# Wider projection streams, split low-rank stores and block-diagonal state products in a two-layer hybrid trunk

## The chip, the cores and the metric

The kernel runs on one core of a Trainium2 chip. The metric is the device time of one execution in microseconds (us). Three executions of the kernel before took 4823.67, 4823.92 and 4831.27 us, median 4823.92. All numbers below that are not one of these come from one further execution, taken with the hardware profiler; it took 4847.04 us, of which 4845.3 us lie between its first and last instruction (the span).

## The reference

Two layers follow each other. Each computes, for 256 context tokens and 2048 latent tokens of width 1024:

```
h  = rms_norm(x, norm_w) * (1 + scale) + shift          # scale, shift, gate from SiLU(c) @ mod_w
pa, pb, pt = split(h @ w_in)                            # 4096 columns: three head groups
ya = rwkv7(pa)      # 6 heads of 64, two directions: per token
                    #   sa = state @ -kk;  state = state * w + sa (x) b + v (x) k;  y = state @ r
                    #   decay and learning rate come through two low-rank maps of width 64
yb = hgrn2(pb)      # 4 heads of 64, two directions, gated linear recurrence
yt = windowed_attention(pt)                             # 6 query heads, 2 key heads, sinks, rotary
x  = x + gate * (concat(ya, yb, yt) @ w_out)
```

In layer 1 the RWKV value is also mixed with that of layer 0. A last RMSNorm ends the trunk. Everything is float32.

## The kernel before

Tokens are numbered 0 to 2303; the first 256 are context. Each layer has two phases.

**Phase 1, the input projection** (`inproj_phase`). `norm_block` normalises 256 tokens, transposes them on TensorE (PE) and writes them as a tile `h` of two parts, a rounded high part and the rest (`hi`, `lo`, type fp32r), with 1024 features along partitions. The weight is taken in tiles of 128 columns (32 in layer 0, 33 in layer 1), in an order `order`, and split the same way on GpSimd (`whi`, `wlo`). A product is 24 matmuls: whi and wlo against the high part and whi against the low part, for 8 slices of 128 features (L347, L348). The tokens go in two sweeps, `SWEEP`: blocks of 512, 256 (context) and 512 tokens, then two of 512. A block of 512 is two runs of 24 matmuls, one for each 256 tokens, into two halves of one PSUM tile `ps` (L344 to L349). ScalarE (ACT) copies `ps` out, VectorE (DVE) applies the centred shift into a tile `s` (two buffers), and `post` does what the column tile needs. Two kinds of column tile matter here:

- j = 9 and j = 10 are the low-rank columns of decay and learning rate, both directions in one tile: partitions 0 to 63 are the forward direction, 64 to 127 the backward one. `parts` (L517 to L529) rounds them into buffers `t` and stores these and the rest to a DRAM scratch `wa`, by DMAs from SyncE's queue (SP).
- j = 3, 4, 5 are RWKV's keys. `post` squares them on ACT into a buffer `t`, sums over heads with a matmul against `bones` into `pa` (L435), and scales with Ln and Exp through two more buffers `t`.

The buffers `t` are four (`CFG["tm"]`). The order of columns begins 9, 3, 10, 4, 0, 5. A preparation of RWKV's chunks (`RwkvPrep`, in windows of 256 tokens) is mixed into phase 1 from the eighth column on.

**Phase 2** (`phase2`) mixes RWKV's 36 chunk steps with HGRN windows, attention blocks and, near its end, the output projection (`Readout`, whose matmuls `opo` stream 512 columns of fp32r). A chunk has 64 tokens; z is the direction, p a pair of heads, hp the head in it. `RwkvSeq.step` is the recurrence: R = KZ against the state S0, `rs` = R + lk on DVE, U = XT against rs, four ACT copies of U into UV, Sn = bkt against UV, the new state on DVE, and the output Y. Before, each of R and U is 12 matmuls, one for each z, p and hp: `t.mm(R[r, z, p], KZ[:, z, 3 + p, hp], S0[:, z, p])`, `t.mm(U[r, z, p], XT[r, z, p], rs[r, z, p])`, where `r` is the head's half of the partitions. `XT` are the inverses of the chunk from the scratch `XD`; `load` fetches them two steps ahead into one of two buffers (L827).

The order on each engine is not the order of the code. A list scheduler with a timeline of its own places each instruction; the emission order, `high_priority` in `step` and the share of each stream in `phase2` steer it. Each engine then works through its list in order, SP's DMA issues too.

Of the kernel before, what the change touches and what calls it, by code (L numbers as in the profile page):

```python
# [46 lines left out]
class Trunk:  # L47
# [185 lines left out]
    def norm_block(self, l, src, tiles, t0, n):  # L233

        nc = self.nc
        h = self.hp.tile([128, 2, KD, BLK + 2], F32R, name="h", tag="h")
        hi, lo = h[:, 0, :, 0:n], h[:, 1, :, 0:n]
        mc = self.modc[l]
        which = 1 if t0 == 0 else 0
        for k in range(0, KD, 2):  # L240
            ps = self.pax.tile([128, 2, n], F32, name="pa", tag="pa")
            hf = self.np.tile([128, 2, n], F32, name="hf", tag="hf", bufs=CFG["hf"])
            for e in range(2):
                for i, x in enumerate(tiles):
                    self.tr(ps[:, e, i * 128:(i + 1) * 128], x[:, (k + e) * 128:(k + e + 1) * 128])
                s, bsh = mc[:, k + e, which, 0:1], mc[:, k + e, which, 1:2]
                self.ts(hf[:, e], ps[:, e], s, ALU.mult, bsh, ALU.add)
            self.act(hi[:, k:k + 2], hf, AF.Identity)
            self.tt(lo[:, k:k + 2], hf, hi[:, k:k + 2].bitcast(F32), ALU.subtract, nc.gpsimd if k >= CFG["nl"] else None)
        if t0 == 0:  # L250

            x, = self.normed(l, src, SWEEP[1][0][0], 2)
            ps = self.pax.tile([128, KD, 2], F32, name="pa", tag="pa")
            for k in range(KD):
                self.tr(ps[:, k], x[:, 128 * k:128 * k + 128])
            hf = self.np.tile([128, KD, 2], F32, name="hf", tag="hf", bufs=CFG["hf"])
            self.tt(hf, ps, mc[:, :, 0, 0:1].to_broadcast([128, KD, 2]), ALU.mult)
            self.tt(hf, hf, mc[:, :, 0, 1:2].to_broadcast([128, KD, 2]), ALU.add)
            hi, lo = h[:, 0], h[:, 1]
            self.act(hi[:, :, n:n + 2], hf, AF.Identity)  # L260
            self.tt(lo[:, :, n:n + 2], hf, hi[:, :, n:n + 2].bitcast(F32), ALU.subtract)
        return hi, lo


    def inproj_phase(self, l, src, prep, start):
# [7 lines left out]
        with ExitStack() as ph:  # L273
            pool = lambda name, bufs, **kw: self.pool(ph, f"{name}{l}", bufs, **kw)
            self.np, self.tmp = pool("np", 1), pool("tm", CFG["tm"])
            wrp, wsp = pool("wr", 1), pool("ws", 2)
            self.hp = pool("hp", 5)
            self.pbp, sbp, kp = pool("pb", 1), pool("sb", 2), pool("keep", 1)
            self.pax = pool("pa", 2, psum=True)
            self.pin = pool("pi", 3, psum=True)  # L280
# [36 lines left out]
            for sw in range(2):  # L317
# [4 lines left out]
                for pos, j in enumerate(order):  # L322
# [16 lines left out]
                    for t0, bn in SWEEP[sw]:  # L339
                        c0, c1 = BLK if skip and t0 == 0 else 0, BLK + 2 if shifted and t0 == 0 else BLK  # L340
                        if c0 >= c1:
                            continue
                        ps = self.pin.tile([128, 512], F32, name="ps", tag="ps")
                        for a in range(0, bn, BLK):  # L344
                            i = 0
                            hh, hl = h[t0 + a]
                            for k, wt, ht in [(k, wt, hh) for k in range(KD) for wt in (hi, lo)] + [(k, hi, hl) for k in range(KD)]:  # L347
                                self.mm(ps[:, a + c0:a + c1], wt[:, k, :], ht[:, k, c0:c1], i == 0, i == 23)  # L348
                                i += 1  # L349
                        if not shifted:  # L350
                            self.evac(l, j, s[:, t0 - base:t0 - base + bn], ps[:, 0:bn], t0 - base, bn)
                        else:
                            o = t0 - base + (1 if t0 == 0 or sw else 2)
                            if c0 == 0:
                                self.act(pb[:, o:o + bn], ps[:, 0:bn], AF.Identity)
                            if t0 == 0:
                                self.act(pb[:, 1282:1283], ps[:, BLK:BLK + 1], AF.Identity)
                        if sw == 0 and pos == len(order) - 1:

                            for _ in range(min(bn // BLK, CFG["ib"], len(todo))):  # L360
                                norm(todo.pop(0))
# [155 lines left out]
    def parts(self, s, base, blks, f):  # L517

        nc = self.nc
        wa = self.scr["wa"].rearrange("z (h p) f t -> h z p f t", h=2)  # L520
        for t0, n in blks:
            sb = s[:, t0 - base:t0 - base + n]
            hi = self.tmp.tile([128, 512], F32R, name="t", tag="t")[:, 0:n]
            nc.vector.tensor_copy(hi, sb)
            for h in range(2):
                nc.sync.dma_start(out=wa[h, :, :, f, t0:t0 + n], in_=hi.bitcast(F32))
            self.tt(sb, sb, hi.bitcast(F32), ALU.subtract)
        lo_t, hi_t = blks[0][0], blks[-1][0] + blks[-1][1]
        nc.sync.dma_start(out=wa[f, :, :, 2, lo_t:hi_t], in_=s[:, lo_t - base:hi_t - base])  # L529

    def tokmajor(self, s, base, blks, name, i):
        nc = self.nc
# [245 lines left out]
class RwkvSeq:  # L778
# [3 lines left out]
    def __init__(self, t, l, ph, prepd):  # L782
        self.t, self.l, self.nc, self.prepd = t, l, t.nc, prepd
        tc, nc, io = t.tc, t.nc, t.io
        st = t.pool(ph, f"rst{l}", 1)
        self.p2 = t.pool(ph, f"rp2{l}", 2)
        self.pp = t.pool(ph, f"rps{l}", CFG["ch"], psum=True)
        self.pq = t.pool(ph, f"rpq{l}", CFG["pq"], psum=True)
        self.mask = st.tile([128, 3, 64], F32, name="rmask")
        nc.sync.dma_start(out=self.mask, in_=io["c_rmask"])  # L790

        self.KZ = [st.tile([128, 2, 6, 2, 64], F32, name=f"KZ{i}") for i in range(2)]
        for a in self.KZ:
            nc.gpsimd.memset(a, 0.0)
        self.S0 = self.T_([128, 2, 3, 64], "S")
        nc.vector.memset(self.S0, 0.0)
        self.ld, self.pr = {}, {}
        self.ahead = CFG["ahead"]
# [11 lines left out]
    def load(self, s):  # L810
        if s >= 36:
            return
        nc, S = self.nc, self.t.scr
        KZ = self.KZ[s % 2]
        q = (nc.sync, nc.scalar, nc.gpsimd)[CFG["rq"]]
        BK = self.T_([128, 2, 3, 128], "BKs")
        XT, UV = self.T_([128, 2, 3, 64], "XTs"), self.T_([128, 2, 3, 128], "UVs")
        for z in range(2):
            c = self.chunk(z, s)
            self.prepd.need(c // 4)  # L820
            q.dma_start(out=BK[:, z], in_=S["KB"][z, c])
            rk = S["RK"][z, c // 4].rearrange("p f (i c) s -> p (f i) c s", c=4)[:, :, c % 4]
            a = 0 if self.out(s) else 3
            for hp in range(2):
                r = slice(64 * hp, 64 * hp + 64)
                q.dma_start(out=KZ[r, z, a:6, hp], in_=rk[r, a:6])
            q.dma_start(out=XT[:, z], in_=S["XD"][z, c // 4, :, :, c % 4])  # L827
            q.dma_start(out=UV[64 * (1 - z):64 * (1 - z) + 64, z], in_=S["vtok"][64 * c:64 * c + 64, :].rearrange("t (p c) -> t p c", c=128))
        self.ld[s] = (BK, KZ, XT, UV)

    def prep(self, s):

        if s >= 36:
            return
        t, nc = self.t, self.nc
        BK, KZ, XT, UV = self.ld[s]
# [32 lines left out]
    def step(self, s):  # L869

        t, nc, l = self.t, self.nc, self.l
        BK, KZ, XT, UV = self.ld.pop(s)
# [4 lines left out]
        units = [(z, p, hp, half[hp]) for z in range(2) for p in range(3) for hp in range(2)]  # L877
        B_ = lambda n: self.pp.tile([128, 2, 3, 64], F32, name=n, tag="R")
        with hi():
            R = B_("R")  # L880
            for z, p, hp, r in units:
                t.mm(R[r, z, p], KZ[:, z, 3 + p, hp], S0[:, z, p])
            rs = lk
            t.tt(rs, R, lk, ALU.add)
        yield
        with hi():
            U = B_("U")
            for z, p, hp, r in units:
                t.mm(U[r, z, p], XT[r, z, p], rs[r, z, p])
            for hp in range(2):  # L890
                for z in range(2):
                    t.act(UV[half[z], z, :, 64 * hp:64 * hp + 64], U[half[hp], z], AF.Identity, scale=-0.5)
        yield
        with hi():
            Sn = B_("Sn")
# [339 lines left out]
def phase2(t, l, prep, pctx, src, dst):  # L1235


    with ExitStack() as ph:
# [58 lines left out]
                   [attn(), left + 48 * 6, 0.0, ae], [readout(), 9 * 6, he, CFG["re"] / 100]]  # L1297
        for s in range(2):
            rw.load(s)
        for _ in rw.prep(0):  # L1300
            pass
        live = [[a, (e - b) / n, b] for a, n, b, e in streams]
# [276 lines left out]
```

## Time and profile before

| | |
|---|---|
| median of three executions | 4823.92 us |
| profiled execution | 4847.04 us, span 4845.3 us |
| PE busy | 4110.6 us (85%) |
| DVE busy | 3202.2 us (66%) |
| ACT busy | 1979.9 us (41%) |
| GpSimd busy | 1373.7 us (28%) |
| phase 1 | about 40 to 1370 us and 2490 to 3780 us |
| phase 2 | about 1370 to 2490 us and 3780 to 4845 us |

Busy is the time in which at least one instruction of the engine was under way. Matmuls overlap, so a busy PE need not be at its peak; the distance from start to start tells its pace. A program matmul on plain float32 operands leaves two MATMUL records (two passes), each with its own weight load; one on fp32r operands, or a transpose, leaves one. The granted PE clock (PEclk) is 1.0 at 2.4 GHz and 0.5 at 1.2 GHz. In a form such as `128*64 128x64` the first pair is the part of the array in use (rows * columns), the second the output partitions' span and the columns streamed.

### The profile page before, as it was taken

The page shows a single profiled execution, that of the slowest core. Times are in us where ns is not written, and L with a number is a line of the kernel's source. Part 1 is how long each engine was busy: PE and PEld are TensorE (multiplying, and loading weights), DVE is VectorE, ACT ScalarE, POOL GpSimd, SP SyncE. Part 2 cuts the span into 40 slices and gives each one's busy share as a digit, 9 for nine tenths or more (in the row PEclk, how much of TensorE's full clock was granted, in tenths as well). Part 3 has the DMA queues.
Part 4 walks back from the last instruction along what each step waited for, and adds up shares of the span by engine and source line. Part 5 has one row for each costly group of instructions (what it writes and reads, how often), then busy time and mean ns, then how long its engine had stood idle before and what let it go on. Part 6 is the DMA issues. An engine that isn't in the chain of part 4 may idle for free. (4 is left out here: it accounts for less than half of the span.)

```text
span 4845.3 us, 109175 instructions
## 1 busy us (share of the span) xinstructions
PE 4110.6 (85%) x44848; PEld 3638.2 (75%) x44848; DVE 3202.2 (66%) x5850; ACT 1979.9 (41%) x4043; POOL 1373.7 (28%) x1304
## 2 busy tenths in 40 slices
PE   7698887788979999877885888977988798999798
PEld 5678886788967777766765878877888677777676
DVE  4337775476676777777852576834775677777787
ACT  3314334343245555543422443242432455545444
POOL 3122122222242233242231222232322333222333
PEclk9799998898989999988987999988999899999899
DMA  5256743366353333335632466423764533333564
GB/s 188 98 185 195 210 149 103 117 213 181 113 164 104 106 105 102 103 105 178 210 121 78 136 213 197 130 93 120 218 189 125 148 92 107 107 95 88 162 192 152
DMA packets 782315, 689.10 MB, mean 142 GB/s; under 512 B 348420, under 2 KB 680004, under 8 KB 781816
## 3 DMA queue, kind: packets, MB, share of 16 engines
q1 hardware_dynamic: 752584, 583.92, 40.0%
q0 software_dynamic: 18720, 68.17, 4.5%
q10 hardware_dynamic: 10512, 30.02, 1.9%
q8 instruction: 355, 5.82, 0.5%
q14 instruction: 144, 1.18, 0.1%
HBM read 440.70 MB, written 241.22 MB: 141 GB/s over the span
## 5 line engine op out<-in xcount | busy, mean ns | idle before, releaser
L67 PE MATMUL ps<-h,whi 128*128 128x256 f32 (+1 forms) x9200 | 1795.9, 294 | 32.0 <-ACT pb L64 12.2
L67 PEld LDWEIGHTS ps<-h,whi 128*128 128x128 f32 x9200 | 1508.1, 199 | 76.6 <-issue 40.6
L67 PE MATMUL ps<-h,wlo 128*128 128x256 f32 (+1 forms) x4600 | 1185.1, 292 | 0.5 <-POOL wlo L74 0.5
L67 PEld LDWEIGHTS ps<-h,wlo 128*128 128x128 f32 x4600 | 913.1, 199 | 17.9 <-issue 15.5
L302 POOL CAST whi<-wraw 128x1024 fp32r<-128x1024 f32 x130 | 161.2, 1240 | 1317.1 <-PE ps L67 1234.1
L74 POOL TENSOR_TENSOR hE<-hb 128x256 f32<-128x256 f32 x408 | 277.6, 703 | 382.7 <-PE wps L67 208.7
L74 POOL TENSOR_TENSOR wlo<-wraw,whi 128x1024 fp32r<-128x1024 f32 x130 | 330.5, 2542 | 10.4
L74 DVE TENSOR_TENSOR hQz<-hE,hqz 64x256 f32<-64x256 f32 x408 | 233.1, 571 | 112.9 <-DMA hqz<-scr_hq 110.1
L1013 DVE COPY_PREDICATED hatt<-lm,wps 64x256 f32<-64x256 int32 x476 | 266.4, 560 | 41.3 <-PE wps L67 33.6
L67 PE MATMUL pq<-KZ,BKs 128*64 128x128 f32 (+1 forms) x1680 | 241.2, 305 | 37.1 <-DMA KZ<-scr_RK 15.7
L74 DVE TENSOR_TENSOR Gs<-can,inv 128x30 f32<-128x30 f32 (+9 forms) x540 | 233.0, 432 | 37.0 <-PE apm L67 25.1
L64 ACT ACT_TABLE_LOAD x170 | 218.1, 1283 | 86.4 <-DVE s L79 32.0
L74 DVE TENSOR_TENSOR inv<-inv,Gs 128x30 f32<-128x30 f32 (+9 forms) x540 | 240.1, 445 | 11.9
L67 PE MATMUL opo<-wohi,ohi 128*128 128x512 f32 x544 | 216.0, 412 | 28.9 <-DVE og L74 25.3
L67 PEld LDWEIGHTS pq<-KZ,BKs 128*64 128x64 f32 (+1 forms) x1680 | 179.9, 177 | 70.7 <-issue 36.7
L64 ACT ACTIVATE s<-ps 128x512 f32<-128x512 f32 x175 | 97.5, 564 | 322.7 <-PE ps L67 303.9
L83 DVE SCALAR_TENSOR_TENSOR s<-pb,par,s 128x1024 f32<-128x1024 f32 (+1 forms) x156 | 213.2, 1370 | 5.5
L64 ACT ACTIVATE pt<-wps 128x512 f32<-128x512 f32 (+1 forms) x288 | 149.5, 525 | 160.6 <-PE wps L71 157.6
L67 PE MATMUL opo<-wolo,ohi 128*128 128x512 f32 x544 | 213.1, 407 | 0.0
L79 DVE TENSOR_SCALAR s<-pb,mu 128x1024 f32<-128x1024 f32 (+1 forms) x78 | 60.8, 779 | 219.4 <-ACT pb L64 136.2
L71 PE MATMUL wps<-ident,prob 128*128 128x128 f32 x960 | 168.8, 292 | 39.7 <-DVE hatt L1013 22.0
L67 PE MATMUL pa<-t,bones 128*128 128x512 f32 (+1 forms) x60 | 40.9, 772 | 184.7 <-ACT t L64 184.7
(265 smaller groups left out, 8709.9 us busy)
## 6 DMA issues: line engine op xcount, KB each, us to landing
wraw<-in_w_in_dram POOLq DMA_DIRECT2D x128, 512.0 KB, 4.5
scr_KB<-tk SPq DMA_DIRECT2D x36, 768.0 KB
BKs<-scr_KB SPq DMA_DIRECT2D x144, 192.0 KB
KZ<-scr_RK SPq DMA_DIRECT2D x272, 96.0 KB
x<-in_mod_w_dram SPq DMA_DIRECT2D x32, 512.0 KB
lkk<-scr_kk SPq DMA_DIRECT2D x36, 384.0 KB
th<-scr_wa SPq DMA_DIRECT2D x36, 384.0 KB
scr_RK<-lkk SPq DMA_DIRECT2D x36, 384.0 KB
```

What stands on the lines that cost most here:

```text
L64: return self.nc.scalar.activation(out=out, in_=in_, func=func, **kw)
L67: return self.nc.tensor.matmul(out=out, lhsT=lhsT, rhs=rhs, start=start, stop=stop)
L71: return self.nc.tensor.transpose(out, in_, self.ident[0:p, 0:p])
L74: return (eng or self.nc.vector).tensor_tensor(out=out, in0=a, in1=b, op=op)
L79: return e.tensor_scalar(out=out, in0=a, scalar1=s1, scalar2=None, op0=op0)
L83: return (eng or self.nc.vector).scalar_tensor_tensor(out=out, in0=a, scalar=s, in1=b, op0=op0, op1=op1)
L302: nc.gpsimd.tensor_copy(hi, w)
L1013: nc.vector.copy_predicated(o, m, d)
```

## The change

Three edits. In the projection, the tile `h` holds 512 tokens (two buffers; the context has its own tile `hc`), and a block of 512 is one run of 24 matmuls of 512 columns. With it, the normalisation of the second sweep's blocks is no longer called after the context's block of the last column. In `parts`, each store to `wa` becomes two, one for each direction. In the recurrence, R and U are 6 matmuls each, one for a pair of heads, with a 128-column stationary operand: for R the two heads' KZ side by side, for U a block-diagonal tile `XZ`, whose off-diagonal blocks stay zero. `XZ` is one buffer, filled for the next step by four DMAs of 64 partitions after this step's U (`inverses`), where before two DMAs filled one of two buffers.

```diff
@@ norm_block
-        h = self.hp.tile([128, 2, KD, BLK + 2], F32R, name="h", tag="h")
-        hi, lo = h[:, 0, :, 0:n], h[:, 1, :, 0:n]
+        if t0 == 0:
+            h = self.hp.tile([128, 2, KD, BLK + 2], F32R, name="hc", tag="hc")
+            c = 0
+        else:
+            c = (t0 - BLK) % (2 * BLK)
+            if c == 0:
+                self.hcur = self.hp.tile([128, 2, KD, 2 * BLK], F32R, name="h", tag="h", bufs=2)
+            h = self.hcur
+        hi, lo = h[:, 0, :, c:c + n], h[:, 1, :, c:c + n]
@@ inproj_phase
-                        for a in range(0, bn, BLK):
-                            i = 0
-                            hh, hl = h[t0 + a]
-                            for k, wt, ht in [...]:
-                                self.mm(ps[:, a + c0:a + c1], wt[:, k, :], ht[:, k, c0:c1], i == 0, i == 23)
-                                i += 1
+                        if bn > BLK:
+                            c1 = bn
+                        hh, hl = h[t0]
+                        i = 0
+                        for k, wt, ht in [...]:
+                            self.mm(ps[:, c0:c1], wt[:, k, :], ht[:, k, c0:c1], i == 0, i == 23)
+                            i += 1
...
-                        if sw == 0 and pos == len(order) - 1:
+                        if sw == 0 and pos == len(order) - 1 and t0 > 0:
@@ parts
-                nc.sync.dma_start(out=wa[h, :, :, f, t0:t0 + n], in_=hi.bitcast(F32))
+                for z in range(2):
+                    nc.sync.dma_start(out=wa[h, z, :, f, t0:t0 + n], in_=hi[64 * z:64 * z + 64].bitcast(F32))
...
-        nc.sync.dma_start(out=wa[f, :, :, 2, lo_t:hi_t], in_=s[:, lo_t - base:hi_t - base])
+        for z in range(2):
+            nc.sync.dma_start(out=wa[f, z, :, 2, lo_t:hi_t], in_=s[64 * z:64 * z + 64, lo_t - base:hi_t - base])
@@ RwkvSeq
-            q.dma_start(out=XT[:, z], in_=S["XD"][z, c // 4, :, :, c % 4])
+    def inverses(self, s):
+        if s < 36:
+            for z in range(2):
+                c = self.chunk(z, s)
+                for hp in range(2):
+                    r = slice(64 * hp, 64 * hp + 64)
+                    self.nc.sync.dma_start(out=self.XZ[r, z, :, hp], in_=self.t.scr["XD"][z, c // 4, r, :, c % 4])
@@ step
-            for z, p, hp, r in units:
-                t.mm(R[r, z, p], KZ[:, z, 3 + p, hp], S0[:, z, p])
+            for z, p in pairs:
+                t.mm(R[:, z, p], KZ[:, z, 3 + p].rearrange("p h s -> p (h s)"), S0[:, z, p])
...
-            for z, p, hp, r in units:
-                t.mm(U[r, z, p], XT[r, z, p], rs[r, z, p])
+            for z, p in pairs:
+                t.mm(U[:, z, p], XT[:, z, p].rearrange("p h s -> p (h s)"), rs[:, z, p])
...
+        self.inverses(s + 1)
```

What the scheduler made of it is shown at three places. The first is SP's queue in layer 0, first sweep, where the low-rank column j = 9 is stored and the keys' stores follow. Before:

```order
L180 DMA x<-in_mod_w_dram 128x1024 x10
L526 DMA scr_wa<-t 2x64x256 x2
L526 DMA scr_wa<-t 2x64x512 x4
L529 DMA scr_wa<-s 2x64x1280
L180 DMA x<-in_mod_w_dram 128x1024 x2
L207 DMA scr_gate<-raw 2x512 x2
L203 DMA mb<-in_mod_b_gate_dram 2x512 x2
L421 DMA scr_k<-s 128x1280
L442 DMA scr_kk<-t 128x256
```

The same place after:

```order
L180 DMA x<-in_mod_w_dram 128x1024 x10
L536 DMA scr_wa<-t 64x256 x4
L536 DMA scr_wa<-t 64x512 x8
L540 DMA scr_wa<-s 64x1280 x2
L430 DMA scr_k<-s 128x1280
L207 DMA scr_gate<-raw 2x512 x2
L180 DMA x<-in_mod_w_dram 128x1024 x2
```

Seven stores whose outermost dimension is the direction (2) have become fourteen whose outermost dimension is 64 partitions; the keys' store follows at once.

The second place is PE in phase 2 of layer 0, around one U; `pq<-AM` and `pq<-KZ,S` are the output product Y of the same step, `wps` belongs to attention and HGRN. Before:

```order
L67 MATMUL U<-lk,XTs 64x64
L67 MATMUL pq<-KZ_13147,S 64x64
L67 MATMUL U<-lk,XTs 64x64
L67 MATMUL pq<-AM,UVs 64x64
L67 MATMUL U<-lk,XTs 64x64
L67 MATMUL wps<-pt,aV 64x128 x7
L67 MATMUL pq<-KZ_13147,S 64x64
L67 MATMUL U<-lk,XTs 64x64
L67 MATMUL pq<-AM,UVs 64x64
L67 MATMUL U<-lk,XTs 64x64 x3
L67 MATMUL wps<-pt,aV 64x128 x3
```

A U in the same phase after:

```order
L67 MATMUL pq<-AM,UVs 64x64
L67 MATMUL U<-lk,XZ 128x64 x6
L67 MATMUL wps<-pt,aV 64x128 x10
L67 MATMUL wps<-hQz_10127,hE_12619 64x64 x8
L67 MATMUL sc<-khi,aqs 128x256
```

U has half the matmuls, each over the whole array, and stands in fewer pieces; over all 72 steps it stood in 188 pieces and R in 189, and now in 152 and 127. From the first R to the last of each layer the array changes its shape between one matmul and the next 1671 times before and 1278 times after (counted over the written order, both layers).

The third place is SP's queue in phase 2, where the inverses are fetched. Before:

```order
L821 DMA BKs<-scr_KB 128x384 x2
L1119 DMA asg<-scr_sga 128x3x128
L826 DMA KZ_13147<-scr_RK 64x6x64 x4
L912 DMA scr_yr<-ys 128x192 x2
L828 DMA UVs<-scr_vtok 64x384 x2
L827 DMA XTs<-scr_XD 128x3x64 x2
```

After:

```order
L936 DMA scr_yr<-ys 128x192 x2
L839 DMA KZ_10095<-scr_RK 64x6x64 x2
L840 DMA UVs<-scr_vtok 64x384
L1143 DMA asg<-scr_sga 128x3x128
L850 DMA XZ<-scr_XD 64x3x64 x4
L973 DMA hk_14300<-scr_hk 128x2x256
L974 DMA hg_15623<-scr_hg 128x2x256
L981 DMA hqz_10119<-scr_hq 64x2x128 x3
```

The two loads of `XTs` have become four of `XZ`, and behind them stand loads of the HGRN stream.

## Rows read from the trace of the kernel before

**Rows 1.** The page: span, then busy time and share of each engine.

```profile
span 4845.3 us, 109175 instructions
PE 4110.6 (85%) x44848; PEld 3638.2 (75%) x44848; DVE 3202.2 (66%) x5850; ACT 1979.9 (41%) x4043; POOL 1373.7 (28%) x1304
```

**Rows 2.** Waits of PE, 0 to 1370 us: who, for whom, total us, times, longest.

```profile
PE pa L67 <- ACT t L64: 85.3, 6, 30.0
PE apm L67 <- DMA daT<-scr_Dx: 35.4, 13, 7.7
```

**Rows 3.** Waits of PE, 2490 to 3780 us.

```profile
PE pa L67 <- ACT t L64: 99.4, 6, 28.6
```

**Rows 4.** Timeline around the first of these waits: PE, ACT, DVE (start, us, instruction, idle before).

```profile
138.63 2.08 PE L67 MATMUL pa<-t,bones 128*128 128x512 f32 x2 [19.89 <-ACT t L64]
137.86 0.72 ACT L64 ACTIVATE t<-s,par 128x512 f32<-128x512 f32 x1 [17.72 <-DMA scr_wa<-t]
150.23 0.54 DVE L79 TENSOR_SCALAR s<-pb,mu 128x256 f32<-128x256 f32 x1 [22.10 <-DMA scr_wa<-s]
```

**Rows 5.** Timeline of SP's queue, 106 to 140 us.

```profile
106.00 18.11 SPq L526 DMA_DIRECT2D scr_wa<-t  x6
124.22 4.94 SPq L529 DMA_DIRECT2D scr_wa<-s  x1
139.17 0.35 SPq L421 DMA_DIRECT2D scr_k<-s  x1
```

**Rows 6.** DMA issues: sizes of the low-rank stores.

```profile
scr_wa<-t SPq DMA_DIRECT2D x32, 256.0 KB
scr_wa<-s SPq DMA_DIRECT2D x4, 640.0 KB
scr_wa<-t SPq DMA_DIRECT2D x8, 128.0 KB
```

**Rows 7.** Windows: us, busy by engine, PEclk, DMA share, GB/s.

```profile
126.00:130.00 4.00, 0.00 (x0) 0.00 (x0) 0.48 (x1) 0.00 (x0) 0.00 (x0) 0.50 0.13 51
140.00:142.00 2.00, 2.00 (x9) 1.50 (x7) 0.00 (x0) 0.21 (x1) 0.00 (x0) 0.50 0.87 335
```

**Rows 8.** Timeline of PE after the wait, to 146 us.

```profile
140.72 0.42 PE L67 MATMUL ps<-h,whi 128*128 128x256 f32 x1
...
144.13 0.41 PE L67 MATMUL ps<-h,whi 128*128 128x256 f32 x1
...
144.53 0.28 PE L67 MATMUL ps<-h,whi 128*128 128x256 f32 x1
...
145.98 1.23 PE L67 MATMUL ps<-h,whi 128*128 128x256 f32 x9
```

**Rows 9.** Groups by form: the projection's 256-column matmuls.

```profile
L67 PE MATMUL ps<-h,whi 128*128 128x256 f32 x8752 | 1709.2, 294 | 31.9 <-ACT pb L64 12.2 <-ACT s L64 9.5 <-ACT h L64 6.6
L67 PE MATMUL ps<-h,wlo 128*128 128x256 f32 x4376 | 1126.1, 292 | 0.5 <-POOL wlo L74 0.5
```

**Rows 10.** Timeline of PE, output projection: 512-column matmuls of fp32r.

```profile
4791.33 0.39 PE L67 MATMUL opo<-wolo,ohi 128*128 128x512 f32 x1
...
4794.09 0.39 PE L67 MATMUL opo<-wolo,ohi 128*128 128x512 f32 x1
```

**Rows 11.** Timeline of PE: 128-column weights, two columns streamed.

```profile
2714.07 0.25 PE L67 MATMUL ps<-h,wlo 128*128 128x2 f32 x1
...
2715.64 0.25 PE L67 MATMUL ps<-h,wlo 128*128 128x2 f32 x1
```

**Rows 12.** Timeline of PE: one R and one U of 12 matmuls in one piece.

```profile
1554.51 0.92 PE L67 MATMUL R<-S,KZ 128*64 128x64 f32 x24 [1.16 <-DVE S L74]
1559.17 0.92 PE L67 MATMUL U<-lk,XTs 64*64 64x64 f32 x24
```

**Rows 13.** Timeline of PE: changes of the array's shape around a piece of R.

```profile
1699.71 0.29 PE L67 MATMUL sc<-khi,aqs 128*128 128x256 f32 x1
1699.83 0.27 PE L67 MATMUL sc<-klo,aqs 128*128 128x256 f32 x1
1700.04 0.68 PE L67 MATMUL R<-S,KZ 128*64 128x64 f32 x14
1700.65 0.44 PE L67 MATMUL sl<-khi,aqs 128*128 128x384 f32 x1
```

**Rows 14.** Windows of phase 2, eight of 200 us (1400 to 2200, 3800 to 4600): sum and mean.

```profile
sum 1600.00, PE 1414.89 PEld 1178.79 DVE 1208.84 ACT 809.05 POOL 496.50; mean PE 176.86 PEld 147.35 DVE 151.11 ACT 101.13 POOL 62.06
```

**Rows 15.** Tile U: the waits of its readers and writers, whole span.

```profile
  DVE lk L74: 25.6, 21
```

**Rows 16.** Waits of SP's queue, whole span.

```profile
SPq L821 <- PE pq L71: 240.8, 49, 11.1
```

More of the change, by code (lines that the diff above doesn't have):

```diff
@@ L261, in norm_block @@
             self.tt(lo[:, :, n:n + 2], hf, hi[:, :, n:n + 2].bitcast(F32), ALU.subtract)
-        return hi, lo
+        return h[:, 0], h[:, 1]
     def inproj_phase(self, l, src, prep, start):
@@ L276, in inproj_phase @@
             wrp, wsp = pool("wr", 1), pool("ws", 2)
-            self.hp = pool("hp", 5)
+            self.hp = pool("hp", 1)
             self.pbp, sbp, kp = pool("pb", 1), pool("sb", 2), pool("keep", 1)
@@ L343, in inproj_phase @@
                         ps = self.pin.tile([128, 512], F32, name="ps", tag="ps")
-                        for a in range(0, bn, BLK):
-                            i = 0
-                            hh, hl = h[t0 + a]
-                            for k, wt, ht in [(k, wt, hh) for k in range(KD) for wt in (hi, lo)] + [(k, hi, hl) for k in range(KD)]:
-                                self.mm(ps[:, a + c0:a + c1], wt[:, k, :], ht[:, k, c0:c1], i == 0, i == 23)
-                                i += 1
+                        if bn > BLK:
+                            c1 = bn
+                        hh, hl = h[t0]
+                        i = 0
+                        for k, wt, ht in [(k, wt, hh) for k in range(KD) for wt in (hi, lo)] + [(k, hi, hl) for k in range(KD)]:
+                            self.mm(ps[:, c0:c1], wt[:, k, :], ht[:, k, c0:c1], i == 0, i == 23)
+                            i += 1
                         if not shifted:
@@ L792, in __init__ @@
         self.KZ = [st.tile([128, 2, 6, 2, 64], F32, name=f"KZ{i}") for i in range(2)]
-        for a in self.KZ:
+        self.XZ = st.tile([128, 2, 3, 2, 64], F32, name="XZ")
+        for a in self.KZ + [self.XZ]:
             nc.gpsimd.memset(a, 0.0)
@@ L816, in load @@
         BK = self.T_([128, 2, 3, 128], "BKs")
-        XT, UV = self.T_([128, 2, 3, 64], "XTs"), self.T_([128, 2, 3, 128], "UVs")
+        UV = self.T_([128, 2, 3, 128], "UVs")
         for z in range(2):
@@ L826, in load @@
                 q.dma_start(out=KZ[r, z, a:6, hp], in_=rk[r, a:6])
-            q.dma_start(out=XT[:, z], in_=S["XD"][z, c // 4, :, :, c % 4])
             q.dma_start(out=UV[64 * (1 - z):64 * (1 - z) + 64, z], in_=S["vtok"][64 * c:64 * c + 64, :].rearrange("t (p c) -> t p c", c=128))
-        self.ld[s] = (BK, KZ, XT, UV)
+        self.ld[s] = (BK, KZ, UV)
+    def inverses(self, s):
[5 more added lines that the diff above has]
+                    self.nc.sync.dma_start(out=self.XZ[r, z, :, hp], in_=self.t.scr["XD"][z, c // 4, r, :, c % 4])
     def prep(self, s):
@@ L835, in prep @@
         t, nc = self.t, self.nc
-        BK, KZ, XT, UV = self.ld[s]
+        BK, KZ, UV = self.ld[s]
         W_ = lambda shape: self.pq.tile(shape, F32, name="pq", tag="pq")
@@ L871, in step @@
         t, nc, l = self.t, self.nc, self.l
-        BK, KZ, XT, UV = self.ld.pop(s)
+        BK, KZ, UV = self.ld.pop(s)
+        XT = self.XZ
         AM, bkt, lk = self.pr.pop(s)
@@ L876, in step @@
         half = (slice(0, 64), slice(64, 128))
-        units = [(z, p, hp, half[hp]) for z in range(2) for p in range(3) for hp in range(2)]
+        pairs = [(z, p) for z in range(2) for p in range(3)]
+        units = [(z, p, hp, half[hp]) for z, p in pairs for hp in range(2)]
         B_ = lambda n: self.pp.tile([128, 2, 3, 64], F32, name=n, tag="R")
@@ L1299, in phase2 @@
             rw.load(s)
+        rw.inverses(0)
         for _ in rw.prep(0):
```

## The prediction

> **What bounds the kernel now.** I read the busy times first: PE is under way for 85% of the span, twice ACT's share [rows 1]. That does not say that PE sets the pace everywhere, so the next view is what PE waited for, in each phase. In both phases 1 the longest item is the same and small in number: the keys' sum over heads, `pa`, waits for ACT's `t`, six times in each layer, 85.3 and 99.4 us in total [rows 2, 3]. Everything else PE waits for there is smaller; the next is 35.4 us [rows 2]. The timeline shows what stands behind the first: PE stood 19.89 us because ACT's square of the keys had waited 17.72 us for a buffer `t` which a store to `wa` still held; DVE lost 22.10 us in the same way to the tile `s` [rows 4]. SP spent 18.11 + 4.94 us to issue the seven stores of that column, where one plain store costs it 0.35 us [rows 5]. And in that stretch the DMA engines were busy for 0.13 of their time at 51 GB/s, that is 2 of 16 engines; a plain 128-partition store two lines on reached 0.87 and 335 GB/s [rows 7]. The store's outermost dimension is the direction, and there are two of them. The column's stores are 2 x 128 KB, 4 x 256 KB and 640 KB [rows 6], 1.97 MB, which at 51 GB/s takes 38.5 us: as long as the whole jam.
>
> Outside these waits, phase 1 is a stream of projection matmuls. Phase 2 is PE-bound more loosely: 176.86 of 200 us busy on the mean, DVE 151.11 [rows 14]. So PE's work counts in both phases, at nearly its price in phase 1 and at about 0.88 of it in phase 2.
>
> **Stores, one direction at a time.** A store of 64 rows can spread over all engines. At the 335 GB/s of [rows 7] the column's data takes 5.9 us instead of 38.5; SP issues fourteen stores at 0.35 us, 4.9 us instead of 23. Then the buffer that held PE for 19.89 us is free some 15 us before it is asked for. What is late next is the keys' own chain of square, sum, Ln and Exp through four buffers; each layer has three key columns of five blocks, 15 in all, and only the six behind a low-rank store appear as waits in [rows 2, 3], so the chain by itself costs PE about nothing. I leave 1.5 us for each of the twelve: -184.7 + 18 = -167. The price at worst is the other end of the evidence, no gain at all if 64 rows spread no better than two.
>
> After a long wait PE's clock is at half: from 140.72 to 144.13 sixteen matmuls of 256 columns took 0.213 us each, from 144.53 to 145.98 twelve took 0.121 [rows 8], at a PEclk of 0.50 in the first part [rows 7]. About 25 records at 0.09 us more are 2.3 us for each wait; most of the twelve are long enough, so -24, with 0 and -30 as ends.
>
> **512 columns at a time.** 65 column tiles by four 512-blocks by 24 are 6240 pairs of 256-column matmuls (12480 of the 13128 in [rows 9]). A pair costs 2 x 0.119 to 0.121 us at full clock: the nine of 145.98 take (1.23 - 0.28)/8 = 0.119 [rows 8]. A 512-column fp32r matmul costs (4794.09 - 4791.33)/12 = 0.230 [rows 10]. The gain is 0.008 to 0.012 us a pair, 50 to 75 us. At half clock I expect none, since 0.213 is already 256 columns at 1.2 GHz. I take 0.008 and 95% at full clock: -48, ends -30 and -70. A block can now start only when both its halves are normalised; at four sweep starts that withholds at most one half block's work, 24 x 0.119 = 2.9 us or double at half clock, and the second sweep's last blocks are normalised later: +6 in all, from 0 to +25.
>
> **R and U.** Before, a product is 24 records that start over 0.92 - 0.22 = 0.70 us [rows 12]: 0.030 us each, because two heads run side by side in two halves of the array. After, it is 12 records, each over the whole array with its own load of 128 columns. The trace has no such matmul with 64 columns streamed, so I bound it. From below: if streaming alone sets the pace, 0.030 us as now, a product takes 0.36 us, and 144 of them gain 0.37 us each, 53 us. In the middle, one record for what was a side-by-side pair, 0.06 us: no change. From above: where 128 columns of four bytes are loaded for two streamed columns, the records are (2715.64 - 2714.07)/14 = 0.112 us apart [rows 11]; there the load alone sets the pace. 12 x 0.112 = 1.34 us against 0.73, 0.61 more, times 144 = +88 us. I take the upper end: this row has the very load in question and almost nothing beside it.
>
> The Trainium skill, "TensorE: Matmul & The Clock Gate", section "LDWEIGHTS (loading the stationary operand)", says that a load costs its columns over 1.2, in ns, whatever the rows: 107 ns for 128 columns. By that an estimate of the term would be 12 x 0.107 = 1.28 us a product, +79 us; the 0.112 of the row agrees with it. The same skill's "TensorEngine Tiling (Array Packing)", section "The Solution", advises what the change gives up: independent tiles for small operands.
>
> Against it stand the changes of the array's shape. `sc` to `sc` is 0.12 us from start to start, `sc` to R 0.21, and from R's last start (1700.04 + 0.68 - 0.22 = 1700.50) to `sl` 0.15 where R to R is 0.06 [rows 13]: 0.09 us for each change. The written order has 393 fewer: -35 us. R and U together: +53 us of PE work, +47 at 0.88.
>
> **The inverses** come into one buffer, so the load of step s + 1 waits on SP for U of step s, and behind it wait loads of HGRN and of the next chunk. A step lasts some 23 us (36 steps in about 830 us, 1370 to 2200) and the load a few, so U should find its data; before, PE's U waited only 25.6 us over the run, for DVE [rows 15]. SP waits elsewhere 4.9 us at a time (240.8/49 [rows 16]). I put +5, ends 0 and the rival below.
>
> **Sum:** -167 - 24 - 48 + 6 + 47 + 5 = -181 us on the profiled 4847.0, that is 4666. The median of the runs shown is 23 us under the profiled one; the same difference from 4823.9 gives 4643, and I say 4640.
>
> **Rivals.**
> 1. *R and U cost no more than before* (the loads hide, or the pace is the stream's). For it: in [rows 12] a pair at 0.06 us already contains two loads. Against it: [rows 11]. The term +47 becomes -31 (shape changes alone) or -77 with the lower bound: 4565 or 4520. The skill's page on TensorE, section "Back-to-back issue gap", has a rule of this kind: 1 to 64 streamed columns cost about 60 cycles, 25 ns, without a word of the load. No row shows it for 128-column weights.
> 2. *The recurrence becomes the bound in phase 2.* R and U lie on the chain from state to state and get 0.6 us longer each; U may wait for XZ too. If each of 72 steps loses 1.5 us more than counted, +108: 4750. For it: the last steps of each layer run with few other streams. Against it: R's and U's waits are small today.
> 3. *The stores do not spread* (the edit does not do what it says). Then the -191 us fall away: 4834. For it only that no 64-row store to `wa` is in the trace. The skill's "DMA: Bandwidth & Descriptors", section "Why a DMA increments its semaphore by 16 and not by 1", speaks against this rival: the engines used are the largest number up to 16 that divides the slowest dimension, 2 before and 16 after; the 0.13 of [rows 7] agrees with the 2.
> 4. *Slower: the single buffer XZ.* The load stands in SP's ordered queue behind stores and loads that wait for other engines, 4.9 us each [rows 16]; if U meets one such wait in every step, 72 x 4.9 = 353 us come on top: 4990. It decides from 184/72 = 2.5 us a step on. Against it: most of a step lies between two Us.
>
> **How the numbers follow.** The forecast as summed has 0.64 with its own range 4595 to 4690; rival 1 has 0.10, rival 2 0.15, rival 3 0.04, rival 4 0.04, and 0.03 is left for what I don't see. The range 4550 to 4735 takes in the upper part of rival 1 and the lower of rival 2. A change of 0.2%, 9.6 us, is about what can be told from none here. Faster by more: the forecast, rival 1, rival 2, and a part of the rest, 0.92. Within it: part of rival 3, 0.02. Slower: 0.06.
>
> **What would show it.** In the profile after: the waits of `pa` for ACT's `t` nearly gone, the low-rank stores issued at about 0.35 us each and the DMA share near them well over 0.13; 6240 projection matmuls of 512 columns 0.23 us apart; R and U records 0.11 us apart, if rival 1 is wrong, and about 0.06 or 0.03, if it is right; phase 1 shorter by about 115 us a layer, phase 2 longer by about 25; no wait of U on `scr_XD` beyond a few us. The prediction is wrong if phase 1 keeps another wait of that size in the same place, if phase 2 grows by over 60 us a layer, or if U waits for XZ in most steps.

## The result

The changed kernel takes 4672.1 us (median of 4 runs, 4661.8 to 4679.3), the kernel before in the same series 4826.0: a ratio of 0.9678, 95% interval [0.9658, 0.9698], or 154 us less. In a second series, beside other kernels, the ratio was 0.9659 [0.9637, 0.9680]. Forecast were 4640, range 4550 to 4735.

The profiled execution after took 4661.8 us, the fastest of its four; that of before, 4847.0, was slower than every other run of its series. So the two traces differ by 185 us, and the medians by 154. I take times from the medians and places from the traces.

The head of the page of after, for [rows 1]:

```profile
span 4660.0 us, 93604 instructions
PE 4070.9 (87%) x36880; PEld 3345.6 (72%) x36880; DVE 3233.3 (69%) x5850; ACT 1972.2 (42%) x4042; POOL 1369.8 (29%) x1306
```

PE's waits in phase 1 of layer 0 (0 to 1330 us), for [rows 2], and then of layer 1 (2400 to 3585 us), for [rows 3]: total us, times, longest.

```profile
PE apm L67 <- DMA daT<-scr_Dx: 35.9, 15, 6.5
PE pa L71 <- DVE hf L80: 26.8, 27, 3.9
...
PE pa L67 <- ACT t L64: 11.6, 5, 7.7
```

```profile
PE pa L71 <- DVE hf L80: 32.2, 27, 9.6
...
PE pa L67 <- ACT t L64: 10.1, 5, 5.2
```

The 184.7 us of `pa` for ACT's `t` are down to 21.7. The wait for `hf` (the norm's tile at the start of a sweep) stood at 15.2 in layer 0 before and is 26.8 now.

SP's queue of after around the first low-rank column, for [rows 5], and then a window there, for [rows 7] (us, busy by engine, PEclk, DMA share, GB/s):

```profile
108.74 9.86 SPq L536 DMA_DIRECT2D scr_wa<-t  x12
118.71 1.17 SPq L540 DMA_DIRECT2D scr_wa<-s  x2
```

```profile
108.00:112.00 4.00, 4.00 (x18) 1.91 (x18) 3.58 (x9) 1.86 (x6) 0.76 (x2) 1.00 0.88 273
```

Fourteen stores are issued in 11 us instead of seven in 23. The DMA share is 0.88 instead of 0.13, and PE is busy all through.

Timeline of PE after: the projection's 512-column matmuls, for [rows 9], and a whole U, for [rows 12].

```profile
329.66 0.39 PE L67 MATMUL ps<-h,wlo 128*128 128x512 f32 x1
...
332.84 0.39 PE L67 MATMUL ps<-h,wlo 128*128 128x512 f32 x1
...
1547.97 1.45 PE L67 MATMUL U<-lk,XZ 128*128 128x64 f32 x12
```

Between the two first rows lie 14 steps: 3.18/14 = 0.227 us each. The twelve records of U start over 1.45 - 0.22 = 1.23 us: 0.112 each. The sum had 0.230 and 0.112.

The same four stretches of before and then of after: phase 1 of layer 0, the rest of layer 0, phase 1 of layer 1, the rest. A phase 1 goes from its first projection matmul to its last. Behind a stretch stand its length and, after the comma, PE's busy time.

```profile
41.00:1335.00 1294.00, 1092.36 (x10132) 1015.56 (x10131) 776.15 (x1330) 455.27 (x722) 325.86 (x280) 0.91 0.50 155
1335.00:2502.00 1167.00, 1004.68 (x12725) 836.43 (x12724) 857.69 (x1653) 535.32 (x1315) 362.49 (x386) 0.93 0.45 130
2502.00:3760.00 1258.00, 1042.97 (x9996) 997.08 (x9996) 749.90 (x1296) 452.03 (x710) 337.18 (x286) 0.90 0.48 148
3760.00:4845.00 1085.00, 952.49 (x11923) 783.83 (x11922) 806.38 (x1522) 522.40 (x1275) 338.73 (x342) 0.94 0.44 128
```

```profile
48.00:1234.00 1186.00, 1042.15 (x7043) 825.99 (x7043) 794.79 (x1322) 445.73 (x714) 327.42 (x277) 0.92 0.54 168
1234.00:2411.00 1177.00, 1031.84 (x11867) 876.93 (x11866) 868.04 (x1664) 539.38 (x1324) 371.96 (x390) 0.92 0.44 130
2411.00:3579.00 1168.00, 1015.84 (x6821) 822.94 (x6821) 751.93 (x1287) 447.50 (x702) 329.84 (x283) 0.91 0.51 158
3579.00:4660.00 1081.00, 957.62 (x11059) 812.45 (x11057) 800.98 (x1522) 521.64 (x1276) 327.56 (x343) 0.92 0.44 128
```

Phase 1 is shorter by 108 and 90 us, the first projection starts 7 us later (48 instead of 41), and phase 2 changes by +10 and -4. Forecast were 115 a layer and +25 a layer. What the engines sat idle for before their instructions on tile `XZ` (us, times), over the whole span of after; DVE's `lk` is U's other operand:

```profile
  DVE lk L74: 33.7, 30
  issue: 0.3, 2
```

No transfer is among U's waits. So the sum came out nearly right; whether each term did, the traces of two kernels can't tell.

### The profile page after: what moved, and what is told of

Read it like the earlier page. It is cut to its first block, busy times and chain, and to the rows that moved or that the text cites. A ratio compares the mean times of both kernels' runs of the same rounds, so it can differ in the third digit from the quotient of the medians.

```text
span 4660.0 us, 93604 instructions
## 1 busy us (share of the span) xinstructions
PE 4070.9 (87%) x36880; PEld 3345.6 (72%) x36880; DVE 3233.3 (69%) x5850; ACT 1972.2 (42%) x4042; POOL 1369.8 (29%) x1306
## 5 line engine op out<-in xcount | busy, mean ns | idle before, releaser
L67 PE MATMUL ps<-h,whi 128*128 128x512 f32 x4160 | 1376.3, 406 | 41.1 <-ACT pb L64 18.6
L67 PEld LDWEIGHTS ps<-h,whi 128*128 128x128 f32 x4160 | 805.5, 195 | 239.7 <-issue 40.8
L67 PE MATMUL ps<-h,wlo 128*128 128x512 f32 x2080 | 849.4, 408 | 0.6 <-issue 0.6
L310 POOL CAST whi<-wraw 128x1024 fp32r<-128x1024 f32 x130 | 151.9, 1168 | 1199.4 <-PE ps L67 1097.6
L67 PEld LDWEIGHTS ps<-h,wlo 128*128 128x128 f32 x2080 | 412.0, 198 | 90.4 <-issue 6.3
L71 PE MATMUL wps<-ident,prob 128*128 128x128 f32 x960 | 169.9, 296 | 45.6 <-DVE hatt L1037 19.9
L83 DVE SCALAR_TENSOR_TENSOR s<-pb,par,s 128x1024 f32<-128x1024 f32 (+1 forms) x156 | 203.5, 1307 | 5.6 <-DVE s L83 0.5
L67 PE MATMUL wps<-hQz,hE 128*64 128x64 f32 (+1 forms) x2992 | 155.8, 246 | 49.3 <-DVE hatt L1037 26.9
L67 PE MATMUL ps<-hc,whi 128*128 128x256 f32 (+2 forms) x880 | 181.2, 293 | 0.8 <-ACT hc L64 0.7
```

The source lines that it names most:

```text
L67: return self.nc.tensor.matmul(out=out, lhsT=lhsT, rhs=rhs, start=start, stop=stop)
L71: return self.nc.tensor.transpose(out, in_, self.ident[0:p, 0:p])
L83: return (eng or self.nc.vector).scalar_tensor_tensor(out=out, in0=a, scalar=s, in1=b, op0=op0, op1=op1)
L310: nc.gpsimd.tensor_copy(hi, w)
```

## The experiments

Each is timed in five rounds beside the kernel before, in three series (before: 4848.7, 4840.5, 4842.8). Ratios are to it, with 95% intervals; 0.001 is 4.8 us. Differences between two kernels carry the two intervals added in squares, some 16 us.

"Halves" means that the first column of each sweep is streamed in two halves of 256 columns. "Old slots" are tiles `h` with a slot for every 256 tokens, so that the second sweep's blocks are normalised when they were in the kernel before.

Each kernel but the change has one trace, and what a trace shows of a stretch varies too: the two traces of the change differ by 15 us in the two phases 1 together, and the two phases 2 last 2231 to 2259 us in the seven kernels that have R and U as before. A difference of that size between two traces is not shown by them alone.

| kernel | median us | ratio | series |
|---|---|---|---|
| stores alone | 4653.6 | 0.9586 [0.9562, 0.9611] | 1 |
| 512 columns alone | 4824.7 | 0.9950 [0.9932, 0.9969] | 1 |
| R and U alone | 4856.8 | 1.0015 [1.0002, 1.0028] | 1 |
| stores and 512 | 4656.2 | 0.9606 [0.9584, 0.9628] | 1 |
| all three (the change) | 4676.7 | 0.9659 [0.9637, 0.9680] | 2 |
| stores, tiles of two blocks, 256 columns | 4644.0 | 0.9580 [0.9555, 0.9605] | 2 |
| stores and 512, old slots, halves | 4615.1 | 0.9529 [0.9504, 0.9554] | 2 |
| stores and 512, halves | 4617.6 | 0.9538 [0.9515, 0.9561] | 3 |
| stores, R and U | 4644.8 | 0.9591 [0.9565, 0.9617] | 3 |
| all three, old slots, halves | 4630.6 | 0.9560 [0.9536, 0.9584] | 3 |
| the change with R twice | 4740.9 | 0.9786 [0.9763, 0.9809] | 2 |

### The parts by themselves

Stores alone (the diff's part in `wa`, on the kernel before):

```
-                nc.sync.dma_start(out=wa[h, :, :, f, t0:t0 + n], in_=hi.bitcast(F32))
+                for z in range(2):
+                    nc.sync.dma_start(out=wa[h, z, :, f, t0:t0 + n], in_=hi[64 * z:64 * z + 64].bitcast(F32))
```

> The kernel before with nothing but the low-rank stores one direction at a time. Theory A (the prediction's terms, each at its size): -167 for the waits and -24 for the clock after them, 4825 - 191 = 4634 us. Theory B (as the traces of before and after read: both phases 1 are together 198 us shorter, with 512 columns in them): the stores bring about 150, 4675 us. Both: the waits of pa for ACT's t fall from 184.7 us to about 20, and phase 2 is as long as before.

Measured: 0.9586, some 200 us [189, 212] less. PE's three longest waits up to 1330 us, and its two phases 1:

```profile
PE apm L67 <- DMA daT<-scr_Dx: 37.5, 13, 7.5
PE aps L67 <- DVE tk L643: 27.6, 10, 4.1
PE pa L71 <- DVE x L79: 16.7, 4, 8.1
```

```profile
44.00:1239.00 1195.00, 1078.00 (x10129) 1004.95 (x10129) 787.60 (x1330) 454.46 (x722) 325.79 (x280) 0.94 0.54 167
...
2410.00:3566.00 1156.00, 1031.92 (x9996) 990.13 (x9995) 753.49 (x1296) 451.18 (x709) 339.43 (x287) 0.93 0.53 161
```

`pa` for `t` is down to 0.4 us there, and in layer 1 (2410 to 3566 us) to one wait:

```profile
PE pa L67 <- ACT t L64: 3.4, 1, 3.4
```

The phases are 2351 us long instead of 2552. PE's busy time in them fell from 2135.3 to 2109.9 with the same matmuls. I put these 25 us down to the clock, since PEclk rose from 0.91 and 0.90 to 0.94 and 0.93; 176 are waits. Theory A stands, and the whole gain of the change is in these two edits.

512 columns alone (the diff's parts in `norm_block` and `inproj_phase`):

```
-                        for a in range(0, bn, BLK):
...
+                        if bn > BLK:
+                            c1 = bn
```

> The kernel before with nothing but the projection at 512 columns. Theory A: -48 for the columns and +6 for the start-ups, 4825 - 42 = 4783 us. Theory B (512 columns gain only the 0.011 us a pair times 6240, 69 us, where PE is not held up otherwise, and the jam behind the stores stays): -30 to -70, 4755 to 4795. A third view, that the later start of each sweep takes more than 25 us, gives 4800 or more. The 19.9 us wait of pa stays in all three.

Measured: 0.9950, 24 us [15, 33] less: short of A and of B, at the bound of the third view. The jam stays, in smaller pieces: 92.1 us in eleven waits where before has 85.3 in six, the first of 16.6 us and not the 19.9 that I expected to stay. PE's waits up to 1330 us:

```profile
PE pa L67 <- ACT t L64: 92.1, 11, 27.3
```

R and U alone (the diff's parts from `XZ` on):

```
-                t.mm(R[r, z, p], KZ[:, z, 3 + p, hp], S0[:, z, p])
+                t.mm(R[:, z, p], KZ[:, z, 3 + p].rearrange("p h s -> p (h s)"), S0[:, z, p])
...
+        self.inverses(s + 1)
```

> The kernel before with nothing but R and U by block-diagonal operands, and the inverses in one buffer. Theory A: +47 for R and U and +5 for the inverses, 4825 + 52 = 4877 us. Theory B (phase 2 did not get longer between the two traces, since the 53 us of added PE work falls into PE's idle time or is outweighed by fewer changes of shape): 0, 4815 to 4835 us. Rival 1 (records no dearer than the pairs that they replace) gives -31, 4794 us; the 0.112 us between records in the trace after speaks against it.

Measured: 1.0015, +7 us [1, 14]. Its two stretches of phase 2:

```profile
1341.00:2514.00 1173.00, 1028.61 (x11862) 874.82 (x11861) 862.11 (x1653) 533.83 (x1315) 365.79 (x386) 0.93 0.44 129
...
3776.00:4863.00 1087.00, 954.95 (x11056) 810.81 (x11056) 809.02 (x1522) 519.92 (x1275) 332.75 (x341) 0.92 0.44 127
```

PE's busy time is 1983.6 where before has 1957.2: 26 us more work, half of the 53 that I put. (In the three other surroundings below, the traces with and without the edit differ by 18 to 42.) The stretches are 8 us longer, which lies within what phase 2 varies by anyway; by the medians 7 of the 26 are paid.

Stores and 512, which is the change with R, U and the inverses taken back:

```
-                t.mm(U[:, z, p], XT[:, z, p].rearrange("p h s -> p (h s)"), rs[:, z, p])
+                t.mm(U[r, z, p], XT[r, z, p], rs[r, z, p])
...
-        self.inverses(s + 1)
```

> The changed kernel with R, U and the inverses as they were before (so: the stores and 512 columns alone). Theory A: 4825 - 233 = 4592 us, 80 us faster than the changed kernel. Theory B: about the time of the changed kernel, 4660 to 4680 us, since R and U cost nothing.

Measured: 0.9606. So 512 columns on top of the stores bring +10 us, within 16 of nothing, and the change loses 26 (plus or minus 15) against this kernel. Theory A's 4592 of 4825, a ratio of 0.952, is missed by 43 us. Its four stretches:

```profile
48.00:1233.00 1185.00, 1046.88 (x7042) 831.27 (x7042) 793.27 (x1323) 446.19 (x714) 327.20 (x277) 0.92 0.56 168
1233.00:2398.00 1165.00, 999.93 (x12729) 831.86 (x12728) 861.59 (x1659) 539.44 (x1322) 366.50 (x389) 0.93 0.45 132
2398.00:3556.00 1158.00, 1010.29 (x6820) 819.18 (x6821) 750.30 (x1288) 448.57 (x704) 329.50 (x282) 0.91 0.53 159
3556.00:4647.00 1091.00, 958.60 (x11924) 788.05 (x11922) 803.33 (x1522) 522.60 (x1275) 334.62 (x344) 0.93 0.44 127
```

Against stores alone PE's busy time in the phases 1 is 53 us less (2057.2 for 2109.9), about as forecast (48), but the phases are only 8 us shorter. The other 45 us are PE waiting, two thirds of it for ACT: 61 us in both phases instead of 31. Half of that is the keys' sum, 18.5 us instead of 3.8 (up to 1330 us, then 2398 to 3556 us):

```profile
PE pa L67 <- ACT t L64: 7.3, 6, 2.3
```

```profile
PE pa L67 <- ACT t L64: 11.2, 5, 6.5
```

### Where the 512 columns' gain went

The change itself, beside the others:

> The changed kernel again, beside the others of this call. Stores and 512 columns alone gave a ratio of 0.9606, R and U alone 1.0015. If R and U cost in the changed kernel what they cost alone, the ratio is 0.962; if they cost what I predicted (+52 us), 0.971; the first comparison of the changed kernel gave 0.9678.

Measured 0.9659: behind stores and 512, R and U cost +26 us (plus or minus 15), where alone they cost 7. Then the tiles of two blocks with matmuls of 256 columns:

```
+                        for a in range(0, bn, BLK):
...
-                            self.mm(ps[:, c0:c1], wt[:, k, :], ht[:, k, c0:c1], i == 0, i == 23)
+                                self.mm(ps[:, a + c0:a + c1], wt[:, k, :], ht[:, k, a + c0:a + c1], i == 0, i == 23)
```

> Stores, and the tiles of h for two blocks with their order of normalising, but matmuls of 256 columns as before; R, U and the inverses as before. So its distance to the stores alone (ratio 0.9586) is the price of the start-ups, and its distance to stores with 512 columns (0.9606) the price of streaming. Theory A (the prediction's terms): start-ups +6, ratio 0.960, and streaming -48 behind it. Theory B (the trace of stores with 512 columns has about 25 us more idle PE at the second sweep of layer 0 than that of stores alone, where PE waits for the norm's tiles hf and x): +25 to +50, ratio 0.964 to 0.969, of which streaming then gives 20 to 40 back. Theory C (512 columns themselves make PE wait for ACT and DVE): start-ups near 0, ratio 0.959, and streaming gives nothing.

Measured 0.9580, as stores alone: tiles and order of normalising cost nothing that shows while a matmul may start on half a tile. Its first projection:

```profile
41.15 0.56 PE L67 MATMUL ps<-h,whi 128*128 128x256 f32 x1
```

That left theory C, or a price that arises only with 512. The next two tell. Old slots and halves:

```
+            self.hAB = [self.hp.tile([128, 2, KD, w], F32R, name=f"h{i}", tag=f"h{i}") for i, w in enumerate((512, 770))]
...
+                    todo = [1280, 1536, 2048, 1792]
...
+                            cuts = [(0, bn)] if pos else [(0, BLK), (BLK, bn)][::-1 if t0 == 1792 else 1]
```

> Stores and 512 columns, R, U and the inverses as before, but h kept in two tiles with slots of 256 tokens (768 and 1024 in one; 256, 512 and the context in the other), so that the second sweep's blocks are normalised in the old order, one of them into the context's slot, and the first column of each sweep taken in halves. Theory A (start-ups cost 6 us): as stores with 512 columns, 0.9606 less 0.001. Theory B (the withheld blocks cost 25 to 50 us): 0.950 to 0.956, faster than the stores alone. Theory C (512 columns make PE wait anyhow): 0.959 to 0.961.

Measured 0.9529: theory B, 37 us under stores and 512. Then the halves alone, in the change's own tiles and order:

```
+                        cuts = [(c0, c1)]
+                        if bn > BLK and pos == 0:
+                            cuts = [(0, BLK), (BLK, bn)]
...
```

> Stores and 512 columns as in the change (R, U, inverses as before), but the first column of each sweep streamed in halves of 256, so that it starts when half a block is normalised; the order of normalising stays the changed one. It tells the two parts of the 37 us between stores with 512 columns (0.9606) and the version with the old order and halves (0.9529) apart. If the withheld half is the cause: 0.953 to 0.955. If the later normalising of the second sweep's blocks is: 0.959 to 0.960, since only the 7 us of the first start come back.

Measured 0.9538: the withheld half is the cause, 33 us (plus or minus 15) for an edit of nothing else; the old order of normalising adds 4, within 17 of nothing. The first projection of stores and 512, and then of this kernel:

```profile
48.21 0.76 PE L67 MATMUL ps<-h,whi 128*128 128x512 f32 x1 [0.27 <-ACT h L64]
```

```profile
41.51 0.56 PE L67 MATMUL ps<-h,whi 128*128 128x256 f32 x1
```

PE's waits around the second sweep of layer 0 (640 to 740 us), of stores and 512, then of this kernel:

```profile
PE pa L71 <- DVE hf L80: 18.7, 10, 4.4
PE pa L71 <- DVE x L79: 5.9, 1, 5.9
PE ps L67 <- ACT h L64: 4.2, 3, 2.6
```

```profile
PE pa L71 <- DVE hf L80: 13.5, 8, 3.9
PE pa L71 <- DVE x L79: 3.7, 1, 3.7
PE ps L67 <- ACT h L64: 2.2, 2, 1.2
```

The first start is 6.7 us earlier, and 9 us of these waits go at the second sweep (7, with the small ones not shown). Its phases 1, and then its phase 2 of layer 1:

```profile
42.00:1215.00 1173.00, 1044.68 (x7154) 836.48 (x7152) 796.21 (x1332) 446.56 (x716) 334.48 (x280) 0.93 0.56 171
...
2385.00:3542.00 1157.00, 1016.57 (x6926) 832.30 (x6925) 757.64 (x1296) 452.16 (x711) 339.10 (x287) 0.91 0.54 160
3542.00:4614.00 1072.00, 949.30 (x11922) 780.94 (x11920) 802.99 (x1522) 521.32 (x1275) 336.04 (x342) 0.94 0.45 129
```

The phases 1 are 13 us shorter together (12 and 1), so with the start the traces show some 20 of the 33 us. The other 13 lie in phase 2: layer 0's is 5 us longer, layer 1's 19 shorter (1072 for 1091), though there ACT and DVE have the same instructions in the same order in both traces, and PE in all but 60 of some 11920 places. So these 13 us are not placed; they are of the size by which phase 2 varies. And even here PE's 49 us less work than with stores alone shorten the phases by 21: more than half is still waiting.

### What R and U cost

Stores with R and U, at 256 columns:

> Stores together with R, U and the inverses, projection at 256 columns as before. Stores alone gave a ratio of 0.9586, R and U alone 1.0015; on top of stores and 512 columns R and U brought 0.9606 to 0.966 or so. If R and U cost the same everywhere (about +8 us), the ratio is 0.960; if they cost more once the jam is gone (+26 us), 0.964; by my prediction's term (+52 us) 0.969.

Measured 0.9591, +2 us over stores alone. The change with old slots and halves:

> The changed kernel with the starts of the sweeps mended (h in slots of 256 tokens in the old order of normalising, first columns in halves). If start-ups and R and U add up, the ratio is that of the changed kernel less 0.0077, 0.958; if R and U cost nothing there, as phase 2 in the traces suggests, 0.953; if their cost grows with what else is taken away, 0.960 or more.

Measured 0.9560, +15 us over the same without R and U. So R and U cost +7, +2, +26 and +15 in four surroundings; alone the interval excludes zero, in the two with 256 columns it is small, and whether it grows with 512 columns stays open at 16 us each.

The traces do not put the +26 where R and U stand. Of the change in the second series:

```profile
48.00:1239.00 1191.00, 1053.35 (x7042) 834.03 (x7042) 792.30 (x1323) 445.76 (x715) 329.24 (x278) 0.91 0.55 167
1239.00:2419.00 1180.00, 1032.99 (x11865) 878.78 (x11865) 868.18 (x1660) 538.39 (x1323) 370.01 (x389) 0.92 0.44 130
2419.00:3597.00 1178.00, 1022.27 (x6821) 829.08 (x6822) 748.07 (x1288) 447.38 (x702) 330.17 (x283) 0.90 0.52 156
3597.00:4675.00 1078.00, 948.57 (x11059) 804.22 (x11057) 809.54 (x1522) 521.02 (x1276) 327.16 (x343) 0.93 0.45 128
```

Phase 2 is 2258 us long in both traces of the change and 2256 in that of stores and 512. Longer is phase 1 of layer 1, 1168 and 1178 us for 1158, in which neither R nor U stands. So the +26 is not shown to be the price of R's and U's work; why phase 1 is longer stays open.

R issued twice, in the change:

```
-            for z, p in pairs:
+            for z, p in pairs + pairs:
                 t.mm(R[:, z, p], KZ[:, z, 3 + p].rearrange("p h s -> p (h s)"), S0[:, z, p])
```

> The changed kernel with each R issued twice (the second writes the same numbers): 72 x 12 more full-array matmuls on the path of the recurrence, 72 x 12 x 0.112 = 97 us of PE work in phase 2. Theory A (PE's work there counts at 0.88): +85 us over the changed kernel. Theory B (PE's idle time of phase 2 takes up a good part, as the kernel with R and U alone suggests: 19 us of 26): +25 to +50 us. Rival 2 (the recurrence is the bound): +97 us or more.

Measured 4740.9, 64 us over the change (plus or minus 15), between A and B. Its two stretches of phase 2:

```profile
1233.00:2446.00 1213.00, 1081.99 (x12298) 930.79 (x12298) 862.47 (x1660) 540.34 (x1324) 364.99 (x389) 0.92 0.43 126
...
3621.00:4740.00 1119.00, 1014.39 (x11489) 868.88 (x11488) 806.89 (x1522) 534.30 (x1283) 322.21 (x342) 0.93 0.43 124
```

PE's busy time is 107 us more than in the change's phase 2 above (115 more than in its trace of the second series), the stretches are 74 longer: a price of 0.64 to 0.69, on the recurrence's own path. Here, unlike with the +26, the time stands in phase 2, in the place of the edit. Rival 2 would have had the stretches longer by all of it.

## Why the prediction was right, and where it was not

**Stores: right, term by term.** -167 for waits and -24 for the clock, measured 176 and 25 in the trace of stores alone. The residue of 1.5 us a wait that I left for the keys' chain was hardly needed there (3.8 us in all); with 512 columns it came back (11.6 + 10.1 us for ten waits in the change). The stores' issue costs 0.82 us each in the change and 0.63 with the stores alone (7.53 us for twelve), not 0.35, without harm. Rival 3 is dead: near the split stores the DMA share is 0.88. This agrees with the Trainium skill, "DMA: Bandwidth & Descriptors", section "Why a DMA increments its semaphore by 16 and not by 1", by which a transfer uses the largest number of engines up to 16 that divides the slowest dimension of both its sides: 16 divides 64.

**512 columns: the work was right, its price was wrong.** PE's work fell by 53 us (48 forecast). That it came so near is in part luck: with the 0.227 us of the trace after in place of 0.230 the same sum gives 65, and PE stood longer at its lower clock (see the last section). The step that failed is "PE's work counts in both phases, at nearly its price in phase 1". Once the jam is gone, PE still waits in many small places for ACT, DVE and transfers, and most of what it saves between them turns into more waits, above all for ACT: 8 of 53 us came out, and 21 of 49 with the sweeps' starts mended. The trace of before had the warning: in its phases 1 PE stood idle for 417 us (2552 less 2135.3), of which only 185 were the jam. Why ACT is later by just that much, no run separates.

**Start-ups: mis-sized.** I priced the withheld half block at 24 matmuls of PE's work, +6 in all, up to 25. It costs 33 (plus or minus 15), of which the traces place some 20: 6.7 at the first start, 13 in the phases 1. My reading, argued and not shown, is that PE can't start and that the norm behind, which goes at DVE's and ACT's pace, has less of PE's work to run beside: around the second sweep the waits for `hf` and `x` are longer, where I counted only the late block.

**R and U: the pace was right, the sum too high, the price too.** A record costs 0.112 us, as forecast. This agrees with the Trainium skill, "TensorE: Matmul & The Clock Gate", section "LDWEIGHTS (loading the stationary operand)", by which a load takes its columns over 1.2, in ns: an estimate of 107 ns for 128. The section "Back-to-back issue gap" of the same page of the Trainium skill gives about 25 ns for 64 streamed columns, but for a matmul by itself: at its head it says that in a stream of loads and matmuls both set the pace, so it does not bear out rival 1 as I had it. But I took 0.030 us before from a clean piece [rows 12]; over all distances inside pieces at full clock of the trace before the mean is 0.037 (48.2 us over 1304 for R, 52.2 over 1401 for U). With it a product takes 12 x 0.112 - 24 x 0.037 = 0.456 us more, and the +88 becomes +66. PE's work rose by 26 instead of 53, so some 40 us went elsewhere, near the 35 put for changes of shape, which no run has by themselves. And the 26 were paid at 7 by the medians alone, where 0.88 was put; twice R paid 0.64 to 0.69. Rival 1's mechanism is refuted. Its time, a term of -31, was not met either: the +2 to +26 measured lie between it and my +47.

**Inverses:** no U waits for the transfer, and rival 4 falls. No run has the single buffer without the new R and U, so if the loads behind it cost something, it stands within theirs.

**The sum** of measured terms: -200 for the stores, +10 for 512 columns with their start-ups, +26 for what R and U add behind both: -164. These are steps from before to the change, so they add up to its second series whatever the causes. Forecast were -191, -42 and +52, -181 in all. The middle term was too good by 52, the last too bad by 26; that they partly cancel is luck, and the range held it.

The best version measured is neither kernel: stores and 512 columns with the first column of each sweep in halves, R and U as before. It takes 4617.6 us, 0.9538 of before, against the change's 0.9659; with old slots it takes 4615.1 (0.9529), which the intervals do not tell apart.

## What to carry to other kernels

Look first at how many DMA engines a transfer on the critical path gets: a store at 0.13 of the engines was worth more than all of the change on PE. Once the one large wait is gone, work saved on PE is worth only what the next waits leave of it, so price it by the idle time between, not by PE's share of the phase. A wider tile also has to be waited for longer: take the first use of it in halves.

## What was not expected of the hardware

In the kernel before, the side-by-side records of R and U mostly start 6 to 7 ns (at least a quarter of them) or 36 to some 100 ns apart, 0.037 us on the mean; a clean piece shows only 0.030. A plain store's issue on SP cost 0.35 us in the kernel before; in the row of twelve after, a store's cost 0.82, and the plain `scr_k` store right behind them 0.87. And kernels with 512-column matmuls ran at a lower granted clock than the stores alone (0.923 for stores and 512, 0.932 for the stores, on the mean of the span), though PE did less: the clock stood at its lower level, 1.2 GHz, for 719 us of the span against 638. What causes this was not tried.
